# Order of the three partial products in a split-precision block, of a pass's first tile, and of four transposes at the start

## The chip, the cores and the metric

The kernel runs on one core of a Trainium2 chip. The metric is device time in microseconds (us) of one execution. The engines are named as the profile names them: PE is TensorE's matmul, PEld its weight load, DVE is VectorE, ACT is ScalarE, POOL is GpSimd, SP is SyncE. Here SP and POOL mostly issue DMA.

## The reference

One encoder layer on a float32 input x of 1024 tokens by 1024 features, weights of float32:

```python
h = swiglu(rmsnorm(x, ffn1_pre_g), ffn1_w_gate, ffn1_w_up, ffn1_w_down)   # 1024 -> 2816 -> 1024
x = x + 0.5 * rmsnorm(h, ffn1_post_g)
qkv = rmsnorm(x, mix_pre_g) @ w_qkv                                       # 16 heads of 64
# 8 heads: 2-D neighbourhood attention; 8 heads: three dilated windows, merged
x = x + rmsnorm(concat([rmsnorm(o_na), rmsnorm(o_dil)]) @ w_out, mix_post_g)
h = swiglu(rmsnorm(x, ffn2_pre_g), ffn2_w_gate, ffn2_w_up, ffn2_w_down)
x = x + 0.5 * rmsnorm(h, ffn2_post_g)
```

`swiglu(x, g, u, d)` is `(silu(x @ g) * (x @ u)) @ d`.

## The kernel before, in words

**Split numbers.** A float32 operand is held as two tiles of TensorE's rounded format: `hi`, the rounded value (an ACT cast), and `lo`, what the rounding lost (a DVE subtraction that reads `hi`). A product is three matmuls: hi times hi, hi times lo, lo times hi. `mm3` (L352) issues them in that order, on lines L354, L355 and L356; each loads its own 128x128 weights. In this kernel the tokens stream as moving operand and the weight columns stand in the array, so L356 is the only one of the three that needs the `lo` part of a weight.

**Seven products.** The large products follow a seven-multiplication scheme of two-by-two blocks. `PairGemm` (L429) does those whose weights stand: the gate and up projections of both feed-forward parts (22 blocks of 128 output columns each) and the q and k projection (8 blocks). `PairGemm.mm` (L457) does one block against one of the seven operands: four k of 128 rows, three matmuls each, so twelve matmuls into one PSUM bank. After the second and the fourth k it calls `c.step()`, which takes one waiting piece of work from each of two lists and issues it there; transposes of the next token tiles get into PE's queue in this way. `PairGemm.ahead` (L489) does the first `early` blocks (11, or all 8 of q and k) against the first two operands before the others exist; in its first turn it uses three blocks that `begin` in `layer` started. `split_left` makes hi and lo of a later block's weights with lines L453 (ACT) and L454 (DVE), called `graw` before and `whi`, `wlo` after. `save` copies a finished block out (L472) and stores it to DRAM (L529, tile `s1d`); the sink adds the second product into the same SBUF tile (DVE, L657), which must wait until that store has read it, and applies Silu (ACT, L659).

**Passes.** `Passes` (L707) does the products whose two sides both stream from DRAM: seven passes over chunks of 128 rows, in groups of up to four chunks (the last may have three or seven). In a group, for each of four token tiles t, it runs over the group's chunks with `mm3` and steps after every second chunk. The chunks' hi and lo (`pw`) are made in pairs on L737 (ACT) and L738 (DVE).

**Operands.** `Operand` (L186) normalises token tiles and transposes them; `one(t)` does half a tile: four PE transposes (L174), an ACT cast to hi, a DVE subtraction to lo, for some tiles a copy that is kept (L261) and stored.

**Order.** PE's instructions stand in the order in which the program issues them. On DVE and ACT a scheduler orders them from the program and its own estimate of when an input is ready; only in the opening (`begin`) are these two also kept in program order. So a new order on PE can move rows on ACT and DVE.

**The opening.** Tiles 0 to 3 are normalised and transposed first. Blocks 0 and 1 start with tiles 0 and 1 alone (256 columns), then take tiles 2 and 3, then block 2 takes all 512 columns. Meanwhile the right halves of the four tiles (operand A12) are transposed: two of them through the step list within block 1, one between blocks 1 and 2, one within block 2. Then `ahead` goes on with A12 for blocks 0 and 1, and with block 3, whose weights are the first that `split_left` makes.

Of the kernel before, what the change touches and what calls it, by code (L numbers as in the profile page):

```python
# [19 lines left out]
P, T = 128, 512  # L20
# [331 lines left out]
def mm3(c, out, ahi, alo, bhi, blo, start, stop, go_on=False):  # L352
    nc = c.nc
    nc.tensor.matmul(out, ahi, bhi, start=start, stop=False, skip_group_check=go_on)  # L354
    nc.tensor.matmul(out, ahi, blo, start=False, stop=False, skip_group_check=go_on)  # L355
    nc.tensor.matmul(out, alo, bhi, start=False, stop=stop, skip_group_check=go_on)  # L356
# [9 lines left out]
def nat_bank(c):  # L366
    return c.psm.tile([P, T], F32, tag="mm", name="accp")
# [61 lines left out]
class PairGemm:  # L429
# [27 lines left out]
    def mm(self, ps, w, i, a, go_on=False, cols=slice(0, T), ks=range(4)):  # L457
        hi, lo = w
        xhi, xlo = self.op.x[a]
        for k in ks:  # L460
            sl = slice(k * P, (k + 1) * P)
            mm3(self.c, ps[:, cols], hi[:, i, sl], lo[:, i, sl], xhi[:, k, cols], xlo[:, k, cols],
                not go_on and k == 0, k == 3, go_on)
            if k % 2:
                self.c.step()

    def bank(self):
        return self.c.psm.tile([P, T], F32, tag="mm", name="mmp")
# [238 lines left out]
class Passes:  # L707
# [35 lines left out]
    def run(self, *which, upto=6):  # L743

        c = self.c
        for p in which:
            chained = PASSES[p][0] in CHAINED
            if not chained:
                self.acc = [None] * 4
            acc, groups = self.acc, self.groups[p]  # L750
            for gi, g in enumerate(groups):
                while self.todo and self.todo[0][0] <= upto and len(self.ready) < len(g) + 3:
                    self.fetch()
                ops = [self.ready.popleft() for _ in g]
                end = gi == len(groups) - 1
                for t in range(4):
                    if acc[t] is None:
                        acc[t] = c.psm.tile([P, T], F32, tag="mm", name="accp")
                    sl = slice(t * P, (t + 1) * P)
                    for j, ((ahi, alo), (bhi, blo)) in enumerate(ops):  # L760
                        mm3(c, acc[t], ahi[:, sl], alo[:, sl], bhi, blo, not chained and gi == 0 and j == 0,
                            end and j == len(ops) - 1, chained)
                        if j % 2:
                            c.step()
                    if end:
                        self.take(p, t, acc[t])
                    c.tick()
# [574 lines left out]
def layer(tc, a, out):  # L1342
    nc = tc.nc
    c = Ctx(tc)
    with ExitStack() as ctx:
# [3 lines left out]
        def sub():  # L1349
            return ctx.enter_context(ExitStack())  # L1350
# [76 lines left out]
        def ffn(which, op, prep, pg, get, turns, sums, more, post, pre, src, dst, begin=None, tables=()):  # L1427
# [131 lines left out]
        with ExitStack() as order:  # L1559
# [16 lines left out]
            op0 = Operand(c, None, 0)  # L1576
# [8 lines left out]
            def begin(pg):  # L1585
# [63 lines left out]
                keeps = []  # L1649
# [13 lines left out]
                acc, s1 = [pg.bank() for _ in range(3)], []  # L1663
# [170 lines left out]
        with ordered():  # L1834
            ops = sub()
# [44 lines left out]
        with ordered():  # L1880
# [113 lines left out]
```

## Time and profile before

| what | us |
|---|---|
| time, median of 3 runs (1842.95 to 1844.0) | 1843.02 |
| the profiled execution: its time | 1842.29 |
| the profiled execution: its span in the trace | 1840.3 |
| PE busy, share of the span | 99% |
| DVE, ACT, POOL busy, share of the span | 72%, 45%, 18% |
| mean granted clock of PE over the span | 0.998 |

The span runs from the first to the last instruction of the program; the execution's time has 2.0 us beside it. A timeline row gives start, length, engine, line, operation, output tile and inputs, and in square brackets how long the engine sat idle before it and what it waited for. A row of waits gives total, number of times and the longest. Matmuls are pipelined, so a row's length is latency; the pace is the distance of starts.

### The profile page before, as it was taken

The numbers are of one execution on the slowest core, as the hardware profiler recorded it, in microseconds if no ns is written. First come the engines' busy times: TensorE is split into PE (matmuls) and PEld (weight loads), VectorE is DVE, ScalarE is ACT, GpSimd is POOL, SyncE is SP. The second block draws the span as 40 slices with busy tenths as digits, with TensorE's granted clock in tenths as the row PEclk, the third lists the DMA queues.
The fourth block names the chain that finished last, engine by engine and source line by source line (L and its number), as shares of the span: only waits on it lengthen the run. The fifth ranks groups of instructions, "written<-read, shape, count | busy, mean of one in ns | idle before, by whom it ended". The sixth has DMA issues, their size and how long they took to land.

```text
span 1840.3 us, 25143 instructions
## 1 busy us (share of the span) xinstructions
PE 1817.0 (99%) x8904; PEld 1527.5 (83%) x8904; DVE 1329.6 (72%) x2243; ACT 829.9 (45%) x1479; POOL 322.4 (18%) x508
## 2 busy tenths in 40 slices
PE   7999999999999999999999999999999999999998
PEld 6887888888888888888899998878888888888886
DVE  5878877776566877477777866778888777754557
ACT  6622233334443657133688765564222333354433
POOL 2223211111121122132333100121111111110000
PEclk9999999999999999999999999999999999999999
DMA  7756565657888857869686532595556566596564
GB/s 274 240 176 226 170 227 208 222 184 252 315 295 314 285 198 260 275 209 305 201 276 217 183 125 94 184 311 183 178 169 212 191 218 233 183 343 204 186 226 150
DMA packets 172991, 409.66 MB, mean 223 GB/s; under 512 B 20081, under 2 KB 42513, under 8 KB 170818
## 3 DMA queue, kind: packets, MB, share of 16 engines
q1 hardware_dynamic: 124706, 246.33, 40.6%
q0 software_dynamic: 47152, 159.64, 23.7%
q10 hardware_dynamic: 1008, 2.10, 0.3%
q8 instruction: 70, 1.15, 0.3%
q14 instruction: 55, 0.45, 0.1%
HBM read 280.49 MB, written 132.56 MB: 224 GB/s over the span
## 4 chain that ended last, share of the span: by engine, by line
PE 89%; DVE 4%; ACT 2%; issue 2%; DMA 2%; POOL 0%; SPq 0%; DVEq 0%; POOLq 0%; ACTq 0%
PE mmp L356 17%; PE mmp L354 17%; PE mmp L355 17%; PE accp L354 10%; PE accp L356 10%; PE accp L355 10%; PE po L1161 2%; PE po L1274 2%; PE ptp L1057 2%; PE trp L174 1%; PE sp L1258 1%; PE sp L1140 1%; DVE pw L738 1%; ACT pb L1049 1%; DMA s1d<-s 0%
## 5 line engine op out<-in xcount | busy, mean ns | idle before, releaser
L354 PE MATMUL mmp<-x,whi 128*128 128x512 f32 (+1 forms) x1464 | 572.7, 391 | 1.7 <-ACT whi L453 1.1
L356 PE MATMUL mmp<-x,wlo 128*128 128x512 f32 (+1 forms) x1464 | 570.2, 389 | 3.8 <-DVE wlo L454 3.8
L355 PE MATMUL mmp<-x,whi 128*128 128x512 f32 (+1 forms) x1464 | 570.1, 389 | 0.5 <-DVE x L182 0.3
L356 PEld LDWEIGHTS mmp<-x,wlo 128*128 128x128 f32 x1464 | 276.2, 189 | 62.2 <-DVE wlo L454 5.5
L354 PEld LDWEIGHTS mmp<-x,whi 128*128 128x128 f32 x1464 | 276.1, 189 | 59.9 <-issue 1.7
L355 PEld LDWEIGHTS mmp<-x,whi 128*128 128x128 f32 x1464 | 276.2, 189 | 56.9 <-DVE x L182 1.2
L738 DVE TENSOR_TENSOR pw<-praw,pw 128x1024 fp32r<-128x1024 f32 (+1 forms) x181 | 200.4, 1151 | 122.4 <-ACT pw L737 121.9
L737 ACT CAST pw<-praw 128x1024 fp32r<-128x1024 f32 (+1 forms) x181 | 168.4, 981 | 204.7 <-PE accp L356 167.7
L354 PE MATMUL accp<-pw 128*128 128x512 f32 x600 | 234.4, 391 | 0.0
L356 PE MATMUL accp<-pw 128*128 128x512 f32 x600 | 233.6, 389 | 0.0
L355 PE MATMUL accp<-pw 128*128 128x512 f32 x600 | 233.5, 389 | 0.0
L453 ACT CAST whi<-wraw 128x1024 fp32r<-128x1024 f32 x126 | 132.4, 1053 | 221.3 <-PE mmp L355 182.9
L454 DVE TENSOR_TENSOR wlo<-wraw,whi 128x1024 fp32r<-128x1024 f32 x126 | 154.6, 1229 | 20.5 <-ACT whi L453 19.2
L356 PEld LDWEIGHTS accp<-pw 128*128 128x128 f32 x600 | 112.6, 188 | 23.5
L355 PEld LDWEIGHTS accp<-pw 128*128 128x128 f32 x600 | 112.7, 188 | 23.2
L354 PEld LDWEIGHTS accp<-pw 128*128 128x128 f32 x600 | 112.7, 188 | 23.2 <-ACT hb L781 0.2
L453 ACT CAST whi<-traw 128x512 fp32r<-128x512 f32 x52 | 32.3, 622 | 157.6 <-DVE traw L545 104.4
L680 POOL DMA_DIRECT2D g<-sg x44 | 23.9, 543 | 428.6 <-DVE sg L673 239.9
L632 DVE TENSOR_TENSOR c<-mmp,u 128x512 f32<-128x512 f32 x52 | 35.9, 691 | 72.8 <-PE mmp L356 72.7
L472 ACT COPY s<-mmp 128x512 f32<-128x512 f32 x52 | 30.6, 588 | 121.3 <-PE mmp L356 113.9
L544 DVE TENSOR_TENSOR wraw<-wraw 128x1024 f32<-128x1024 f32 x52 | 63.6, 1223 | 13.1 <-DMA wraw<-in_wu_dram 12.2
L619 DVE TENSOR_TENSOR c<-mmp,v 128x512 f32<-128x512 f32 x52 | 35.7, 686 | 32.5 <-PE mmp L356 32.5
(286 smaller groups left out, 2775.4 us busy)
## 6 DMA issues: line engine op xcount, KB each, us to landing
praw<-g SPq DMA_DIRECT2D x70, 512.0 KB, 5.7
wraw<-in_wg_dram SPq DMA_DIRECT2D x44, 512.0 KB, 4.2
wraw<-in_wu_dram SPq DMA_DIRECT2D x44, 512.0 KB, 6.8
tr<-in_wd_dram SPq DMA_DIRECT2D x44, 512.0 KB, 6.6
g<-sg POOLq DMA_DIRECT2D x88, 256.0 KB, 5.0
ts<-tr POOLq DMA_DIRECT2D x22, 1024.0 KB, 4.7
praw<-ts SPq DMA_DIRECT2D x88, 256.0 KB, 3.8
praw<-in_wd_dram SPq DMA_DIRECT2D x66, 256.0 KB, 5.6
```

Source lines behind the costliest of these rows:

```text
L354: nc.tensor.matmul(out, ahi, bhi, start=start, stop=False, skip_group_check=go_on)
L355: nc.tensor.matmul(out, ahi, blo, start=False, stop=False, skip_group_check=go_on)
L356: nc.tensor.matmul(out, alo, bhi, start=False, stop=stop, skip_group_check=go_on)
L453: nc.scalar.copy(hi, raw)
L454: nc.vector.tensor_sub(lo, raw, hi.bitcast(F32))
L544: nc.vector.tensor_sub(r[:, 0:2], r[:, 1:3], r[:, 0:2])
L632: c.behind(lambda: nc.vector.tensor_add(c21, d, u2), *((DVE,) if self.sink.soon and b == self.n - 1 else ()))
L737: nc.scalar.copy(hi, raw[:, :m])
L738: nc.vector.tensor_sub(lo, raw[:, :m], hi.bitcast(F32))
L1057: nc.tensor.transpose(ps[:, j, :], src[:, j * P:(j + 1) * P], c.ident)
L1161: nc.tensor.matmul(po[:, un * 2 + j], pt[:, 2 * j + t, :], rhs, start=t == 0, stop=t == 1)
L1274: nc.tensor.matmul(po[0][:, u], pt[0][:, j, :], vs[:, k0 + j, :], start=j == 0, stop=j == n - 1)
```

## The change

It has three parts. In `PairGemm.mm` the twelve matmuls of a block are issued as eight with the `hi` weight (for each k: times x hi, times x lo) and then four with the `lo` weight. The first step comes after k = 1 of the `hi` ones, so after four matmuls in place of six; the second after all twelve, as before. In `Passes.run` the first token tile (t = 0) of a group takes its chunks two at a time: both chunks' hi times hi, both hi times lo, both lo times hi, with a step after each two and one more after an odd last chunk; the other three tiles are as before. In the opening, `one(2)` and `one(3)` of the right halves go into the step list of block 2 together, where `one(2)` was issued ahead of block 2.

```diff
     def mm(self, ps, w, i, a, go_on=False, cols=slice(0, T), ks=range(4)):
...
         for k in ks:
             sl = slice(k * P, (k + 1) * P)
-            mm3(self.c, ps[:, cols], hi[:, i, sl], lo[:, i, sl], xhi[:, k, cols], xlo[:, k, cols],
-                not go_on and k == 0, k == 3, go_on)
-            if k % 2:
+            mm(out, hi[:, i, sl], xhi[:, k, cols], start=not go_on and k == 0, stop=False, skip_group_check=go_on)
+            mm(out, hi[:, i, sl], xlo[:, k, cols], start=False, stop=False, skip_group_check=go_on)
+            if k == 1:
                 self.c.step()
+        for k in ks:
+            sl = slice(k * P, (k + 1) * P)
+            mm(out, lo[:, i, sl], xhi[:, k, cols], start=False, stop=k == 3, skip_group_check=go_on)
+        if 3 in ks:
+            self.c.step()
...
-                    for j, ((ahi, alo), (bhi, blo)) in enumerate(ops):
-                        mm3(c, acc[t], ahi[:, sl], alo[:, sl], bhi, blo, not chained and gi == 0 and j == 0,
-                            end and j == len(ops) - 1, chained)
-                        if j % 2:
+                    n = 2 if t == 0 else 1
+                    for j in range(0, len(ops), n):
+                        two = [(a[:, sl], b) for i in (0, 1, 2) for (ahi, alo), (bhi, blo) in ops[j:j + n]
+                               for a, b in [((ahi, bhi), (ahi, blo), (alo, bhi))[i]]]
+                        for i, (a, b) in enumerate(two):
+                            c.nc.tensor.matmul(acc[t], a, b, start=not chained and gi == 0 and j == i == 0,
+                                               stop=end and j + n >= len(ops) and i == len(two) - 1,
+                                               skip_group_check=chained)
+                        if n == 2 or j % 2:
                             c.step()
...
                 for b in range(3):
-                    if b == 1:
-                        c.steps.extend(lambda t=t: op0.one(t) for t in range(2))
-                    elif b:
-                        op0.one(2, keeps)
-                        c.steps.append(lambda: op0.one(3, keeps))
+                    if b:
+                        c.steps.extend(lambda t=t: op0.one(t, *([keeps] if t > 1 else [])) for t in (2 * b - 2, 2 * b - 1))
                     pg.mm(acc[b], pg.w[b], 0, A11, cols=slice(256 if b < 2 else 0, 512))
```

In the changed kernel L463 and L464 are the matmuls with the `hi` weight (L354 and L355 before) and L469 those with the `lo` weight (L356). Outside the touched functions' lines, its line numbers are higher by 6, later by 11 or 8: L657 and L659 become L663 and L665.

**First place: PE in the opening, end of block 2** (`x_161`, `x_162` are hi and lo of operand A11; `x_163`, `x_164` those of A12; `trp` is a transpose's output). Before, from the transposes of tile 3:

```order
L174 MATMUL trp<-ident,x 128x128 x4
L354 MATMUL mmp<-x_161,whi 128x512
L355 MATMUL mmp<-x_162,whi 128x512
L356 MATMUL mmp<-x_161,wlo 128x512
L354 MATMUL mmp<-x_161,whi 128x512
L355 MATMUL mmp<-x_162,whi 128x512
L356 MATMUL mmp<-x_161,wlo 128x512
L354 MATMUL mmp<-x_163,whi 128x512
L355 MATMUL mmp<-x_164,whi 128x512
```

With the change, from the transposes of tile 2:

```order
L174 MATMUL trp<-ident,x 128x128 x4
L463 MATMUL mmp<-x_161,whi 128x512
L464 MATMUL mmp<-x_162,whi 128x512
L463 MATMUL mmp<-x_161,whi 128x512
L464 MATMUL mmp<-x_162,whi 128x512
L469 MATMUL mmp<-x_161,wlo 128x512 x4
L174 MATMUL trp<-ident,x 128x128 x4
L463 MATMUL mmp<-x_163,whi 128x512
L464 MATMUL mmp<-x_164,whi 128x512
```

Tile 3's transposes moved behind block 2's last matmul, straight ahead of the first matmul that reads all of A12; the six matmuls that stood between them now stand ahead.

**Second place: ACT, a few instructions later** (`s_362` and `s_399` are the saved blocks 0 and 1; the first `whi<-graw` is block 3, the second block 4; L166 takes the squares of token tiles 4 and 5, then 6). Before:

```order
L261 COPY raw<-trp 128x512 x2
L166 ACTIVATE xn,ss<-x 128x1024 x2
L659 ACT_TABLE_LOAD
L659 ACTIVATE s_362<-s_362 128x512
L453 CAST whi<-graw 128x1024
L659 ACTIVATE s_399<-s_399 128x512
L166 ACTIVATE xn,ss<-x 128x1024
L453 CAST whi<-graw 128x1024
```

With the change:

```order
L261 COPY raw<-trp 128x512 x2
L166 ACTIVATE xn,ss<-x 128x1024 x2
L453 CAST whi<-graw 128x1024
L665 ACT_TABLE_LOAD
L665 ACTIVATE s_362<-s_362 128x512
L453 CAST whi<-graw 128x1024
L665 ACTIVATE s_399<-s_399 128x512
L166 ACTIVATE xn,ss<-x 128x1024
```

Block 3's cast moved ahead of a table load and the first Silu, block 4's ahead of the second Silu and a square.

**Third place: DVE, the same stretch** (L157 to L159 are steps of the reciprocal root for tiles 4 and 5, L226 scales these tiles). Before:

```order
L158 TENSOR_TENSOR e<-e,y 128x2
L657 TENSOR_TENSOR s_399<-mmp,s_399 128x512
L159 SCALAR_TENSOR_TENSOR y<-e,y 128x2
L226 SCALAR_TENSOR_TENSOR xn<-x,y,gain 128x1024
L454 TENSOR_TENSOR wlo<-graw,whi 128x1024
L226 SCALAR_TENSOR_TENSOR xn<-x,y,gain 128x1024
L454 TENSOR_TENSOR wlo<-graw,whi 128x1024
```

With the change:

```order
L151 TENSOR_SCALAR y<-y 128x2
L454 TENSOR_TENSOR wlo<-graw,whi 128x1024
L157 TENSOR_TENSOR e<-y,v 128x2
L158 TENSOR_TENSOR e<-e,y 128x2
L159 SCALAR_TENSOR_TENSOR y<-e,y 128x2
L663 TENSOR_TENSOR s_399<-mmp,s_399 128x512
```

Block 3's subtraction moved from behind the addition into `s_399` and one scaling to a place ahead of the iteration and of that addition.

More of the change, by code (lines that the diff above doesn't have):

```diff
@@ L459, in mm @@
         xhi, xlo = self.op.x[a]
+        mm, out = self.c.nc.tensor.matmul, ps[:, cols]
         for k in ks:
             sl = slice(k * P, (k + 1) * P)
-            mm3(self.c, ps[:, cols], hi[:, i, sl], lo[:, i, sl], xhi[:, k, cols], xlo[:, k, cols],
-                not go_on and k == 0, k == 3, go_on)
-            if k % 2:
+            mm(out, hi[:, i, sl], xhi[:, k, cols], start=not go_on and k == 0, stop=False, skip_group_check=go_on)
+            mm(out, hi[:, i, sl], xlo[:, k, cols], start=False, stop=False, skip_group_check=go_on)
+            if k == 1:
                 self.c.step()
+        for k in ks:
[3 more added lines that the diff above has]
+            self.c.step()
     def bank(self):
```

## The prediction

> **What bounds the kernel now.** I read the page's first part, then PE's waits, then one steady stretch by windows.
>
> ```profile
> PE 1817.0 (99%) x8904; PEld 1527.5 (83%) x8904; DVE 1329.6 (72%) x2243; ACT 829.9 (45%) x1479; POOL 322.4 (18%) x508
> PE mmp L356 <- DVE wlo L454: 3.8, 4, 2.6
> PE mmp L354 <- ACT whi L453: 1.1, 1, 1.1
> PE trp L174 <- ACT raw L261: 0.5, 1, 0.5
> L354 PE MATMUL mmp<-x,whi 128*128 128x512 f32 x1448 | 567.0, 392 | 1.1 <-ACT whi L453 1.1
> 1400.00:1500.00 100.00, 100.00 (x443) 82.83 (x442) 74.91 (x93) 34.25 (x46) 15.15 (x26) 1.00 0.62 216
> ```
>
> PE is busy for 99% of the span. The rows of waits give total, times and longest; the two `mmp` rows are the largest that an engine causes, 3.8 and 1.1 us. The window shows the rest: 443 matmuls in 100 us, so 0.226 us from start to start, at a granted clock of 1.00 (the number after POOL's). The other engines have slack. So a change can save only where PE stands still or its pace changes, and PE's stops of this kind lie in few places. The largest is at the opening:
>
> ```profile
> 32.56 0.39 PE L356 MATMUL mmp<-x,wlo 128*128 128x512 f32 x1
> 32.94 1.03 ACT L453 CAST whi<-graw 128x1024 fp32r<-128x1024 f32 x1
> 34.02 0.50 PE L354 MATMUL mmp<-x,whi 128*128 128x512 f32 x1 [1.06 <-ACT whi L453]
> 34.04 0.69 DVE L657 TENSOR_TENSOR s<-mmp,s 128x512 f32<-128x512 f32 x1 [0.77 <-DMA s1d<-s]
> 34.35 0.40 PE L355 MATMUL mmp<-x,whi 128*128 128x512 f32 x1
> 34.83 1.28 DVE L226 SCALAR_TENSOR_TENSOR xn<-x,y,gain 128x1024 f32<-128x1024 f32 x1
> 36.03 1.22 DVE L454 TENSOR_TENSOR wlo<-graw,whi 128x1024 fp32r<-128x1024 f32 x1
> 37.31 0.50 PE L356 MATMUL mmp<-x,wlo 128*128 128x512 f32 x1 [2.56 <-DVE wlo L454]
> 37.64 0.39 PE L354 MATMUL mmp<-x,whi 128*128 128x512 f32 x1
> 41.98 0.40 PE L354 MATMUL mmp<-x,whi 128*128 128x512 f32 x1
> 44.94 0.39 PE L355 MATMUL mmp<-x,whi 128*128 128x512 f32 x1
> ```
>
> Starts 0.226 apart are the pace; what is over it is lost. From 32.56 to 34.02 PE loses 1.23 us: block 3's first matmul waits for its ACT cast, which began only at 32.94. The second matmul comes 0.33 later, so 0.10 is lost in restarting. Then the first `lo` matmul is due at 34.58 and starts at 37.31: 2.73 lost, and 0.10 again behind it. The brackets show less idle time (1.06, 2.56), because the last matmul's latency counts as busy; so a wait costs its bracket and about 0.27. Why `lo` is late stands in the DVE rows: an addition into `s` waited 0.77 us for the store that reads this tile, and the scaling at 34.83 and the subtraction at 36.03 are queued behind it. From 37.64 to 41.98 are twelve starts, 2.72 us at the pace, but 4.34 passed: 1.62 more. Windows of 3.4 us say why (columns: us, busy of PE, PEld, DVE, ACT, POOL, then clock):
>
> ```profile
> 30.70:34.10 3.40, 2.33 (x11) 1.60 (x10) 2.12 (x13) 3.24 (x5) 1.15 (x3) 1.00 1.03 421
> 34.10:37.50 3.40, 0.84 (x3) 0.41 (x4) 3.37 (x5) 2.61 (x4) 1.02 (x2) 1.00 1.02 369
> 37.50:40.90 3.40, 3.40 (x11) 2.66 (x11) 2.09 (x2) 0.10 (x1) 0.00 (x0) 0.63 1.03 411
> ```
>
> After a stretch with PE busy for only 0.84 of 3.40 us the granted clock fell to 0.63. The stop at 34.02 to 37.31 is paid twice. All this sums to 1.23 + 0.10 + 2.73 + 0.10 + 1.62 = 5.8 us.
>
> The Trainium skill ("TensorE: Matmul & The Clock Gate", Part 1) says that the clock halves after an idle window of about 3.4 us, free-running, and warns of gaps over about 3.4 us. The trace does not agree in the size: a gap of 2.56 us idle, with few matmuls around it, was enough here. By the rule alone the 1.62 us would not be there to win and the sum below would be 5.3 us in place of 6.9; the measurement decides.
>
> **The change, part by part: the opening.** The order rows put tile 3's transposes behind block 2. What that costs is worked out from these rows:
>
> ```profile
> 23.54 0.42 PEld L174 LDWEIGHTS trp<-ident,x 128*128 128x128 f32 x4 [0.26 <-ACT raw L261]
> 25.42 0.60 PE L174 MATMUL trp<-ident,x 128*128 128x128 f32 x4
> 25.77 0.48 PE L354 MATMUL mmp<-x,whi 128*128 128x512 f32 x1
> 26.05 0.59 ACT L181 CAST x<-trp 128x512 fp32r<-128x512 f32 x1 [0.44 <-PE trp L174]
> 25.88 1.49 DVE L182 TENSOR_TENSOR x<-trp,x 128x512 fp32r<-128x512 f32 x2
> 27.25 0.39 PE L354 MATMUL mmp<-x,whi 128*128 128x512 f32 x1
> 27.47 0.45 PE L355 MATMUL mmp<-x,whi 128*128 128x512 f32 x1
> ```
>
> Up to the first A12 matmul (27.25) PE does the same work in both kernels. Tile 2's transposes waited 0.26 us at 23.54 for their PSUM buffer's copy; they now come four matmuls later, so this goes. Tile 3's slot is 0.35 (25.42 to 25.77). So in the changed kernel tile 3's transposes start at 27.25 - 0.26 - 0.35 = 26.64. Their output was there 0.63 after the start (26.05 - 25.42), the cast takes 0.59, and a subtraction 0.69 (25.88 + 1.49 = 27.37 is the end of two), with 0.10 to the matmul that reads it (27.47). That gives 27.27, 27.90, and with 0.03 between cast and subtraction 28.62 for the second's end: the first A12 matmul starts near 27.9, the second near 28.7, against 27.47 before. **This part costs 1.2 us**: a wait for the cast and one for the subtraction, in place of a wait of 0.2. Behind PE nothing is lost that isn't counted; on ACT the next copies, squares and block 3's cast stand behind the cast:
>
> ```profile
> 27.93 1.08 ACT L261 COPY raw<-trp 128x512 f32<-128x512 f32 x2
> 28.88 1.09 ACT L166 ACTIVATE xn<-x 128x1024 f32<-128x1024 f32 x1
> 30.88 0.21 ACT L166 ACTIVATION_READ_ACCUMULATOR xn<-x 128x1 f32 x1
> 31.11 1.28 ACT L659 ACT_TABLE_LOAD   x1
> 32.40 0.63 ACT L659 ACTIVATE s<-s 128x512 f32<-128x512 f32 x1
> graw<-in_wg_dram SPq DMA_DIRECT2D x1, 512.0 KB, 8.0
> ```
>
> The copies (1.08) follow a save (0.59, like the cast) and then begin at 28.5, not 27.93; the squares end near 31.7, not 31.09. In the changed order block 3's cast comes next, ahead of table load (1.28) and Silu (0.63). Its data, issued at 23.50, landed 8.0 us later, at 31.5. So `hi` is ready at 31.7 + 1.03 = 32.7, and `lo` (1.22, no longer behind the addition) at 34.0. PE reaches block 3 after 24 matmuls of A12: 28.7 + 0.10 + 23 x 0.226 = 34.0, its first `lo` eight later, 35.8. Both are in time, by 1.3 and 1.8 us, and this holds down to the next ones: block 4's cast follows the Silu (32.7 + 1.28 + 0.63 + 1.03 = 35.7, needed at 39.4). With no stop near 34 I expect no fall of the clock. Counting block 3's first matmul as one, the row at 44.94 is the 29th (12 of block 3, 12 of block 2's A12, 5 of block 4). Without the transposes that now stand shortly ahead of it, it starts at 34.0 + 28 x 0.226 = 40.3. **The opening gains 4.6 us**, the 5.8 less 1.2.
>
> **Three waits for `lo` later.** Each stands at a block's third matmul:
>
> ```profile
> 690.24 0.50 PE L356 MATMUL mmp<-x,wlo 128*128 128x512 f32 x1 [0.15 <-DVE wlo L454]
> 1202.56 0.50 PE L356 MATMUL mmp<-x,wlo 128*128 128x512 f32 x1 [0.40 <-DVE wlo L454]
> 1231.72 0.50 PE L356 MATMUL mmp<-x,wlo 128*128 128x512 f32 x1 [0.70 <-DVE wlo L454]
> 1230.45 1.22 DVE L454 TENSOR_TENSOR wlo<-graw,whi 128x1024 fp32r<-128x1024 f32 x1
> ```
>
> `lo` is now read six matmuls later, 6 x 0.226 = 1.36 us. The losses are the brackets and 0.27 each: 0.42, 0.67 and 0.97. All are below 1.36, so all three go, **2.1 us**. The third is the closest: PE arrives there earlier by the 0.67 saved just before, while the `lo` at 1230.45 hangs on a chain that I can't shift for sure; but the changed DVE order also puts it ahead of one 128x512 subtraction (0.69 in the row at 34.04), which pays that back.
>
> **A pass's first tile.**
>
> ```profile
> 733.30 0.39 PE L356 MATMUL mmp<-x,wlo 128*128 128x512 f32 x1
> 733.53 0.39 PE L354 MATMUL accp<-pw,x 128*128 128x512 f32 x1
> 734.52 0.50 PE L355 MATMUL accp<-pw,x 128*128 128x512 f32 x1 [0.61 <-DVE pw L738]
> ```
>
> The second matmul waits for `pw`'s `lo`; due at 733.76, it lost 0.76. One `hi` matmul now stands between: **0.23 us** gained. The rows of waits name no other pass that waits for an operand, so the pairs give nothing elsewhere: their `lo` is made while the group before is multiplied.
>
> **Moved for nothing.** A put's first half comes two matmuls (0.45 us) earlier, one in the last group before q and k comes six earlier, and some neighbours on ACT, DVE, SP (two loads of `wu` ahead of `wd`) and POOL change places. I take 0. The nearest row is the 0.5 us that one transpose waited for an ACT copy, the only such wait of an operand's put behind the opening; that one stays, since neither its place nor its ACT neighbours change. The other puts' tiles were scaled in time, which is what hides the move. If that cover failed in all eleven first halves it would cost 11 x 0.45 = 5.0 us; a swap of neighbours gives or costs at most one 0.69 row where PE waits for it, and I know of no such place but the one above.
>
> **Sum.** 4.6 + 2.1 + 0.2 = 6.9 us off the profiled execution's own 1842.29 (1840.3 of span and 2.0 around it): 1835.4. The median of the runs shown is 0.7 above that execution, so I predict **1836.1**.
>
> **Rivals.**
> - *The clock falls anyway.* The new waits at 27.9 and 28.7 stop PE for some 1.2 us. Against it: the window 30.70 to 34.10 had PE busy for 2.33 of 3.40 and the next one still started at clock 1.00. For it: the window's phase isn't in my hands. Price 1.6: 1837.7.
> - *Block 3's `hi` takes the place of `lo`.* If copies and squares run later than I have them, PE waits for the cast; it is in front of table load and Silu for certain, so the loss is at most the 1.23 of before and some restart, perhaps again at block 4: 1.5 to 2.5 lost, 1837.6 to 1838.6.
> - *The gain is given back.* The opening runs ahead, but the puts that come earlier find their tiles not yet scaled, and pay the 5.0 above: 6.9 - 5.0 = 1.9 is left, 1841.1, no difference. For it: the tiles are scaled on DVE, the second busiest engine (72%). Against it: none but the one put waited.
> - *Slower: the pace.* The change touches 3 x 1448 matmuls of full width in blocks. If eight with `hi` and four with `lo` run at another distance than 0.226, the whole span moves: 1.6 ns more each eats the 6.9, and from 2.4 ns on the kernel is slower by over 0.2% (3.7 us); at 2.5 ns it costs 10.9: 1847.0. Against it: from 733.30 to 733.53, from a `lo` weight to a `hi` one of another product, it is 0.23 like the mean of the window, in which same and other weights follow each other; and there is one weight load for each matmul (8904 of both), so no load repeats more or less than before.
> - *It doesn't do what it says.* PE would have to wait at the first `hi` matmul for `lo` as well; the order of PE's rows names `lo` only in the last four. Chance 0.
>
> **How the numbers follow.** Forecast 0.68, clock 0.08, `hi` in place of `lo` 0.09, given back 0.12, pace 0.03. Faster by over 0.2%, which is about what a measurement here can tell from no change, covers the first three: 0.85; within it 0.12; slower 0.03. The range reaches from 1834.0 (the opening's wait half as long, a put's 0.5 gone, the run-to-run spread) up to 1839.8, which takes in the clock and the late `hi`, and leaves out most of the last two.
>
> **What would show it.** Right: no PE wait for `wlo` or `whi` at blocks; two new short ones near 28 us, for L181 and L182; clock 1.00 throughout 30 to 42 us; the 29th matmul above at about 40.8 with the transposes ahead of it, not 44.94; the pace still 442 or 443 matmuls in 100 us. Wrong: a clock below 1 in the opening, a wait for `whi` near 34, a new wait at puts, or 440 matmuls in 100 us.

## The result, and the profile after

The changed kernel took 1837.24 us (median of 8 runs, 1836.51 to 1840.07), the kernel before 1843.0 (8 runs, 1840.68 to 1844.82): a ratio of 0.9969, 95% interval 0.996 to 0.9978. It is faster by 5.8 us, where 6.9 were forecast; 1836.1 was forecast and 1834.0 to 1839.8 was the range. Two further comparisons of the same kernel gave 0.9963 (0.9951 to 0.9976) and 0.9971 (0.996 to 0.9981).

The first part of the page and PE's waits (total, times, longest) in the changed kernel:

```profile
PE 1814.7 (99%) x8904; PEld 1525.1 (83%) x8904; DVE 1323.8 (72%) x2243; ACT 834.5 (45%) x1479; POOL 323.5 (18%) x508
```
```profile
PE mmp L463 <- ACT x L181: 1.3, 2, 0.7
PE mmp L463 <- DVE v L606: 1.1, 1, 1.1
...
PE mmp L464 <- DVE x L182: 0.6, 2, 0.4
```

No wait for a block's `whi` or `wlo` is left. The rows with L181 and L182 count two waits each: one stood before the change too, between 11 and 20 us, and the other is the one that the forecast put near 28 us. The row with `v` (L606) was not forecast. The pace did not move; the same steady window as before:

```profile
1400.00:1500.00 100.00, 100.00 (x443) 82.80 (x442) 74.10 (x92) 35.11 (x46) 14.60 (x25) 1.00 0.62 221
```

The opening in the timeline, PE's rows and the ACT and DVE rows that make block 3's weight:

```profile
26.57 0.51 PE L463 MATMUL mmp<-x,whi 128*128 128x512 f32 x1 [0.67 <-ACT x L181]
27.29 0.50 PE L464 MATMUL mmp<-x,whi 128*128 128x512 f32 x1 [0.22 <-DVE x L182]
30.69 1.05 ACT L453 CAST whi<-graw 128x1024 fp32r<-128x1024 f32 x1 [0.63 <-DMA graw<-in_wg_dram]
31.76 1.28 ACT L665 ACT_TABLE_LOAD   x1
31.77 1.22 DVE L454 TENSOR_TENSOR wlo<-graw,whi 128x1024 fp32r<-128x1024 f32 x1 [0.48 <-ACT whi L453]
32.64 0.39 PE L463 MATMUL mmp<-x,whi 128*128 128x512 f32 x1
34.45 1.07 PE L469 MATMUL mmp<-x,wlo 128*128 128x512 f32 x4
41.98 0.50 PE L463 MATMUL mmp<-x,whi 128*128 128x512 f32 x1
```

The cast starts at 30.69, when its data is there, ahead of the table load at 31.76; `wlo` ends at 32.99. PE reaches block 3 at 32.64 and its first `wlo` matmul at 34.45, and waits for neither. The matmul at 41.98 comes about 0.35 late, behind a copy of a bank (L478) that itself waited for a store; this was not forecast (0.50 and 0.39 in the two repeats). The clock (the number after POOL's) stays at 1.00:

```profile
34.00:37.40 3.40, 3.40 (x17) 2.82 (x15) 3.23 (x10) 2.19 (x4) 1.59 (x3) 1.00 1.00 374
37.40:40.80 3.40, 3.40 (x18) 2.83 (x17) 1.87 (x3) 0.00 (x0) 0.00 (x0) 1.00 1.02 411
```

To see where the time came from, I count PE's matmuls and transposes in order and take the time from the start of one to the start of another, at places where all kernels have done the same work. Each column is one stretch (from the n-th to the m-th; the first is counted from the span's start, and the last column is the start of the last one); the names are explained with the experiments below. `before 2` is a second profile of the kernel before; `after`, `after 2` and `after 3` are three of the changed one.

```
us, from n       0     44   2000   3004   3048   6100   6228   6260   8700
      to m      44    200   2100   3048   3240   6148   6260   6444   8790   last start
before       18.91  36.95  22.75   9.53  42.69  11.82   7.26  40.08  20.40      1832.40
before 2     18.67  37.39  23.22   9.56  42.69  11.80   6.92  40.09  21.08      1833.42
after        17.59  32.68  23.42   9.12  42.48  11.08   6.27  41.88  21.32      1828.09
after 2      18.07  32.92  22.67   9.47  42.47  11.10   6.27  42.04  20.71      1827.06
after 3      17.67  32.68  22.81   9.12  42.48  11.11   6.27  42.27  21.17      1827.54
e1           17.73  34.80  23.61   9.12  42.51  11.09   6.27  42.34  20.94      1830.07
e2           18.75  32.29  23.03   9.57  42.69  11.80   7.32  40.09  21.14      1829.54
e4           17.94  35.20  22.91   9.55  42.70  11.80   7.05  40.09  21.10      1829.99
f4           18.80  32.58  22.99   9.11  42.49  11.09   6.27  42.48  21.14      1828.93
g2           18.83  32.28  23.38   9.11  42.48  11.09   7.52  40.81  21.18      1828.51
g3           18.19  32.79  23.23   9.43  42.47  11.09   8.09  40.32  21.24      1828.52
h1           18.22  32.81  24.37   9.11  42.48  11.09   6.27  40.84  20.40      1827.54
h2           17.75  32.27  23.44   9.43  42.47  11.11   6.27  41.40  21.17      1828.00
```

Means of the three profiles after less the two before: start -1.01, opening (44 to 200) -4.41, the wait at 690 -0.31, the pass's first tile -0.22, the waits at 1202 and 1231 -0.71 and -0.82, then **+1.98** in the stretch behind them (6260 to 6444, 1235 to 1275 us of before). All else, the long steady stretches included, is +0.15. The sum is -5.35, of the profiles; the runs' medians differ by 5.8, with an interval of 4.1 to 7.4.

The start's -1.01 does not come from the change. The trace records the granted clock only from where it first rises to 1.00, at 15.31 us in `after`; a window ahead of that reads 1.00 because nothing is recorded there. Up to that point PE runs at half pace (rows at the end of this document), and the start follows the time of the rise in all 13 profiles (us):

```
              after 3  after     h2     e1     e4  after 2     g3     h1  before 2  before     g2     e2     f4
clock rises     15.19  15.31  15.73  15.79  16.05    16.50  16.56  16.70     17.60   17.91  18.00  18.13  18.31
44th starts     17.67  17.59  17.75  17.73  17.94    18.07  18.19  18.22     18.67   18.91  18.83  18.75  18.80
```

Kernels with the old order of the products rise early (e4) and late (e2), and so do those with the new one. In g2, whose opening is the changed kernel's, and in e2, which has its puts, the clock rose as late as in the kernel before. Their start and opening together take 51.11 and 51.04, the kernel before 55.86 and 56.06: 4.9 less, where the means above give 5.4. By this estimate some 4.8 of the 5.35 are the change's.

### The profile page after: what moved, and what is told of

It reads as the page before. It is cut to its first block, busy times and chain, and to the rows that moved or that the text cites. A ratio compares the mean times of both kernels' runs of the same rounds, so it can differ in the third digit from the quotient of the medians.

```text
span 1836.0 us, 25149 instructions
## 1 busy us (share of the span) xinstructions
PE 1814.7 (99%) x8904; PEld 1525.1 (83%) x8904; DVE 1323.8 (72%) x2243; ACT 834.5 (45%) x1479; POOL 323.5 (18%) x508
## 3 DMA queue, kind: packets, MB, share of 16 engines
q8 instruction: 70, 1.15, 0.2%
## 4 chain that ended last, share of the span: by engine, by line
PE 57%; issue 29%; DVE 4%; POOL 3%; DMA 3%; ACT 2%; POOLq 0%; SPq 0%; DVEq 0%; ACTq 0%
PE accp L771 13%; PE mmp L463 10%; PE mmp L464 10%; PE mmp L469 10%; PE po L1172 2%; PE po L1285 2%; PE ptp L1068 2%; PE accp L354 1%; PE accp L356 1%; PE accp L355 1%; POOL g L710 1%; PE sp L1269 1%; DVE pw L744 1%; PE sp L1151 1%; PE trp L174 1%
## 5 line engine op out<-in xcount | busy, mean ns | idle before, releaser
L463 PE MATMUL mmp<-x,whi 128*128 128x512 f32 (+1 forms) x1464 | 571.8, 391 | 2.6 <-ACT x L181 1.3
L464 PE MATMUL mmp<-x,whi 128*128 128x512 f32 (+1 forms) x1464 | 569.0, 389 | 0.7 <-DVE x L182 0.6
L771 PE MATMUL accp<-pw 128*128 128x512 f32 x1800 | 411.6, 390 | 1.1 <-DVE hb L805 0.6
L469 PE MATMUL mmp<-x,wlo 128*128 128x512 f32 (+1 forms) x1464 | 390.3, 388 | 0.0
L463 PEld LDWEIGHTS mmp<-x,whi 128*128 128x128 f32 x1464 | 275.6, 188 | 61.7 <-ACT x L181 2.2
L464 PEld LDWEIGHTS mmp<-x,whi 128*128 128x128 f32 x1464 | 275.7, 188 | 57.2 <-DVE x L182 1.6
L469 PEld LDWEIGHTS mmp<-x,wlo 128*128 128x128 f32 x1464 | 274.5, 188 | 56.7
L453 ACT CAST whi<-wraw 128x1024 fp32r<-128x1024 f32 x126 | 132.5, 1052 | 180.2 <-PE mmp L464 166.2
L453 ACT CAST whi<-traw 128x512 fp32r<-128x512 f32 x52 | 32.3, 621 | 135.2 <-DVE traw L551 91.5
L478 ACT COPY s<-mmp 128x512 f32<-128x512 f32 x52 | 30.6, 589 | 133.0 <-PE mmp L469 121.3
L771 PE MATMUL accp<-pw,x 128*128 128x512 f32 x312 | 71.9, 390 | 0.4 <-DVE pw L744 0.4
L771 PEld LDWEIGHTS accp<-pw,x 128*128 128x128 f32 x312 | 58.3, 188 | 12.8 <-DVE pw L744 0.8
L625 DVE TENSOR_TENSOR c<-mmp,v 128x512 f32<-128x512 f32 x52 | 35.8, 689 | 36.9 <-PE mmp L469 36.9
L1285 PE MATMUL po<-vs,pt 128*128 128x128 f32 x352 | 49.9, 276 | 0.0
L1068 PE MATMUL ptp<-ident,pb 128*128 128x128 f32 x304 | 48.9, 272 | 0.0
```

The lines of the kernel that those rows point to most:

```text
L453: nc.scalar.copy(hi, raw)
L463: mm(out, hi[:, i, sl], xhi[:, k, cols], start=not go_on and k == 0, stop=False, skip_group_check=go_on)
L464: mm(out, hi[:, i, sl], xlo[:, k, cols], start=False, stop=False, skip_group_check=go_on)
L469: mm(out, lo[:, i, sl], xhi[:, k, cols], start=False, stop=k == 3, skip_group_check=go_on)
L771: c.nc.tensor.matmul(acc[t], a, b, start=not chained and gi == 0 and j == i == 0, stop=end and j + n >= len(ops) and i == len(two) - 1, sk ...
L1068: nc.tensor.transpose(ps[:, j, :], src[:, j * P:(j + 1) * P], c.ident)
```

## The experiments

**e1 and e2: the change in two halves.** A put is the transposes of one token tile with what ACT and DVE make of their output; head's puts are those of the right halves in the opening. e1 is the changed kernel with head's puts as before; e2 is the kernel before with head's puts as changed, that is, the same edit the other way round:

```diff
-                    if b:
-                        c.steps.extend(lambda t=t: op0.one(t, *([keeps] if t > 1 else [])) for t in (2 * b - 2, 2 * b - 1))
+                    if b == 1:
+                        c.steps.extend(lambda t=t: op0.one(t) for t in range(2))
+                    elif b:
+                        op0.one(2, keeps)
+                        c.steps.append(lambda: op0.one(3, keeps))
```

> The changed kernel with head's puts as before (tile 2 ahead of block 2's first product, tile 3 at its first step); the new order of the products and of a pass's first tile stays. ACT and DVE then have the order of the kernel before around block 3. Theory A (the puts' place, through the order on ACT and DVE, is what saves the opening): PE still waits about 1.2 us for block 3's whi near 34 us, and for wlo about 1.35 in place of 2.73, since lo is read six matmuls later; with the 2.1 of the three later waits and 0.2 of a pass's first tile that is 3.7 us below the kernel before if the clock falls again, 5.3 if it doesn't (ratio 0.998 or 0.997). Theory B (the later reading of lo saves the opening by itself): no wait near 34, 8.1 us below (ratio 0.9956).

> The kernel before with head's puts in the new place alone; products and passes in the old order. ACT and DVE have the changed kernel's order around block 3. Theory A: no wait for whi near 34, the clock stays at 1.00, tile 3's new waits near 28 us cost 1.2; the opening gains about 4.3, less up to 0.5 where lo is read six matmuls earlier; the three later waits for wlo (0.42, 0.67, 0.97 lost) stay: 3.8 to 4.3 us below the kernel before, ratio 0.9978. Theory B: the stop near 34 to 37 stays, and tile 3's 1.2 comes on top: 1.2 us slower, ratio 1.0007.

e1 took 0.9978 (0.9969 to 0.9986) of the kernel before, 3.7 us less; e2 0.9977 (0.9966 to 0.9987), 4.1 less. PE's rows in e1's opening with a wait, and the windows around the second:

```profile
32.74 0.50 PE L463 MATMUL mmp<-x,whi 128*128 128x512 f32 x1 [1.09 <-ACT whi L453]
36.92 1.20 PE L469 MATMUL mmp<-x,wlo 128*128 128x512 f32 x4 [2.07 <-DVE wlo L454]
```
```profile
34.00:37.40 3.40, 1.33 (x6) 0.82 (x5) 3.36 (x5) 2.60 (x4) 0.72 (x2) 1.00 1.03 383
37.40:40.80 3.40, 3.40 (x17) 2.79 (x16) 1.79 (x2) 0.58 (x1) 0.34 (x1) 1.00 1.03 402
```

And in e2's:

```profile
27.70 0.50 PE L354 MATMUL mmp<-x,whi 128*128 128x512 f32 x1 [0.67 <-ACT x L181]
28.42 0.50 PE L355 MATMUL mmp<-x,whi 128*128 128x512 f32 x1 [0.22 <-DVE x L182]
```

In e1 the waits for `whi` and `wlo` are both there, though `wlo` is read six matmuls later; in e2 neither is, though it is read as early as before. So the stop at block 3 goes by the puts' place, through the order that it gives ACT and DVE. Theory B falls. Two details of e1 were not as expected: `wlo` was late by 2.07 and not 1.35, since PE came to block 3 at 32.74 in place of 34.02 while `wlo` came only 0.4 earlier (36.9 for 37.3); and the clock stayed at 1.00. That e1 saved the 3.7 of theory A is partly luck: this figure was for a clock that falls (5.3 if it doesn't), and it had no term for the stretch from 6260, which is 2.3 longer here. In the table the opening is 2.4 shorter in e1, 4.9 in e2 and 4.4 in the whole change. The +1.98 stands in e1 (42.34) and not in e2 (40.09): it belongs to the new order of the products or of the passes, not to the puts.

**e4: the kernel before, with only the order on ACT and DVE changed** at block 3 (no matmul moves; `own` holds the last ACT and DVE instruction behind the split):

```diff
-                self.sink.first(b, a, True, s1, tie)
+                with ExitStack() as st:
+                    for i in own if b < len(begun) - 1 else ():
+                        st.enter_context(c.tc.issue_after(i))
+                    self.sink.first(b, a, True, s1, tie)
             c.tick()
+            if begun and b == 0:
+                c.behind(lambda: self.split_left(len(begun)), ACT)
+                own = [next(i for i in reversed(nc.cur_bb.bb.instructions) if i.engine == e) for e in (ACT, DVE)]
```

> The kernel before, with only block 3's cast and subtraction ordered ahead of the first Silus on ACT and of the first additions into s on DVE; no matmul moves. Theory A: whi is there at about 32.7, wlo at about 34.0; PE loses about 0.7 at the third matmul of block 3 and some restart in place of 4.2, the clock stays at 1.00: 4.9 us below the kernel before, ratio 0.9973. Theory B (the order on ACT and DVE matters little, the products' order does): no difference, ratio 1.000.

It took 0.9986 (0.9977 to 0.9995), 2.7 us less: half of it. PE's waits, and the ACT rows behind the second:

```profile
33.40 0.50 PE L356 MATMUL mmp<-x,wlo 128*128 128x512 f32 x1 [0.53 <-DVE wlo L454]
...
44.84 0.50 PE L354 MATMUL mmp<-x,whi 128*128 128x512 f32 x1 [2.52 <-ACT s L472]
```
```profile
33.52 1.06 ACT L453 CAST whi<-graw 128x1024 fp32r<-128x1024 f32 x1 [1.43 <-DMA graw<-in_wg_dram]
34.59 1.28 ACT L666 ACT_TABLE_LOAD   x1
...
44.20 0.59 ACT L472 COPY s<-mmp 128x512 f32<-128x512 f32 x1 [1.83 <-DMA sgd<-s]
```

The first half is as expected: the `whi` wait is gone, the `wlo` wait is 0.53, the clock stayed at 1.00. But the tie was too strong: block 4's cast went ahead of the table load too, and the first Silu came at 35.89 in place of 32.40. Its store left later, and a copy into the same tile (44.20) waited for it; PE lost 2.77 there. With no matmul moved, the order on ACT and DVE took away one stop of this size and made another.

**Repeats: e3 and i1, the changed kernel again; g4, the kernel before again.**

> The changed kernel as it is, for a second profile. Theory A: the opening repeats (no wait near 34, clock 1.00 from 30 to 42); the new waits of the first profile at 474.98 (0.46 idle), 1266.89 (1.15) and 1798.22 (0.64) hang on when transfers land; those that hang on the program's order repeat within 0.1, those that hang on how transfers meet come and go. Theory C (all of them belong to the change): all three repeat, and the time stays 4.3 us below the profiled execution of the kernel before.

> The changed kernel as it is, beside the other two on one chip, and for a third profile. The waits for L181 and L182 near 27, near 42 (0.3 to 0.5) and for v near 1266 (1.1 to 1.2 idle) repeat; those for hb near 475 and 1798 may be there or not (both kernels have shown them and not shown them).

> The kernel before as it is, for a second profile. Theory A: the waits at 34.02 (whi), 37.31 (wlo), 690.24, 1202.56 and 1231.72 repeat within 0.2, since they follow from the order on the engines; the clock falls again behind the stop near 37, as it did in the first profile (1.6 us). Theory H (the fall hangs on the phase of the clock's own windows, not on the stop alone): the stop is there and the clock stays at 1.00, with twelve starts behind it in 2.7 us in place of 4.3. The wait for the hb copy near 475 to 480 and near 1800 is absent, since PE comes there later.

(g4 took 0.9999 of the kernel before, 0.9989 to 1.0009.) In before, all five waits repeat, two of them not within the 0.2 that I gave (2.98 in place of 2.56 near 37, 0.37 in place of 0.70 near 1232), and the clock falls again. These two windows are the clock's own: in the trace's records it rises at 17.60 us, falls at 38.08 and rises at 41.49, that is, 6 and 7 times 3.413 us behind the first rise.

```profile
34.67:38.07 3.40, 0.57 (x3) 0.48 (x3) 3.36 (x5) 2.67 (x4) 0.63 (x2) 1.00 1.04 386
38.08:41.49 3.41, 3.41 (x10) 2.63 (x9) 1.70 (x2) 0.00 (x0) 0.00 (x0) 0.50 1.02 412
```

Theory H stays open: the first rise was at 17.91 and 17.60 in the two profiles, so the clock's windows lay nearly alike, and no profile shows this stop with another phase.

In the changed kernel the waits near 27 and 1266 repeat (for `v`: 1.15, 1.15 and 0.82 idle), and so does the small one near 42 (idle for 0.25 in the second profile, too short to be listed in the other two). The waits for `hb`, the tile that takes a pass's finished banks, near 475 and 1798 come and go; the kernel before has them in its second profile too (480.52, idle for 0.26), where I had expected none. They do not belong to the change, and theory C falls for them.

**g2 and h1: where the 1.98 comes from.** In this stretch the last early blocks of the second feed-forward part run, with the last put (token tile 7) among them. L310 is a subtraction of that put, for operand S3; L295 casts an operand's hi, L296 subtracts for its lo. `sg` is a block's Silu, `sgd` its copy in DRAM, `tr<-in_wd_dram` a load of `wd`, and `v` an SBUF tile to which DVE adds a finished bank. Rows of the changed kernel:

```profile
1250.45 1.28 DVE L296 TENSOR_TENSOR x<-s,x 128x512 fp32r<-128x512 f32 x2
1251.66 0.68 DVE L310 TENSOR_TENSOR s<-x,s 128x512 f32<-128x512 f32 x1
1252.37 0.63 ACT L295 CAST x<-s 128x512 fp32r<-128x512 f32 x1 [1.04 <-DVE s L310]
1252.91 0.58 ACT L665 ACTIVATE sg<-mmp 128x512 f32<-128x512 f32 x1
1253.02 0.55 SPq L413 DMA_DIRECT2D tr<-in_wd_dram  x1
1253.79 0.54 POOL L669 DMA_DIRECT2D sgd<-sg  x1 [1.61 <-ACT sg L665]
1260.17 0.60 ACT L665 ACTIVATE sg<-mmp 128x512 f32<-128x512 f32 x1 [1.98 <-DMA sgd<-sg]
1261.73 1.23 DVE L454 TENSOR_TENSOR wlo<-wraw,whi 128x1024 fp32r<-128x1024 f32 x1 [2.29 <-ACT whi L453]
1266.06 0.68 DVE L606 TENSOR_TENSOR v<-mmp,u 128x512 f32<-128x512 f32 x1
1266.89 0.47 PE L463 MATMUL mmp<-x,whi 128*128 128x512 f32 x1 [1.15 <-DVE v L606]
```

and of the kernel before, for the same work:

```profile
1255.73 0.68 DVE L310 TENSOR_TENSOR s<-x,s 128x512 f32<-128x512 f32 x1
1256.93 1.89 DVE L296 TENSOR_TENSOR x<-s,x 128x512 fp32r<-128x512 f32 x3
1258.30 0.54 POOL L663 DMA_DIRECT2D sgd<-sg  x1 [2.72 <-ACT sg L659]
1259.49 0.55 SPq L413 DMA_DIRECT2D tr<-in_wd_dram  x1
```

Before, the put's subtraction L310 stands ahead of the L296 subtractions. In the changed kernel it stands behind three of them; its ACT cast, which is ahead of the Silu, waits 1.04 for it, so the Silu's store is issued behind the two loads of `wd` and not ahead of them. It lands after 6.3 us (the changed kernel, first line) in place of 2.3 (before):

```profile
DMA to landing us min/median/max: 6.3/6.3/6.3
```
```profile
DMA to landing us min/median/max: 2.3/2.3/2.3
```

The later Silu at 1260.17 waits 1.98 for that tile, the cast and the `wlo` behind it are late, `v` is added late on DVE, and PE waits 1.15 for `v`'s bank. All 13 profiles agree: in the five with the store behind the loads it lands after 6.0 to 6.4 us, in the eight with the store ahead after 2.3. g2 issues that subtraction early in every put; h1 does the same under `if t == 7`, for the last tile alone:

```diff
-        c.sums.extend([lambda: (sub(s2, s1, a11), split(S2, s2)), lambda: split(S1, s1),
-                       lambda: (sub(a21, a11, a21), split(S3, a21)), end])
+        c.sums.extend([lambda: (sub(s2, s1, a11), sub(a21, a11, a21), split(S2, s2)), lambda: split(S1, s1),
+                       lambda: split(S3, a21), end])
```

> The changed kernel; in the second half of a put of tiles 4 to 7 the subtraction for S3 (L310) is issued right behind the one for S2 (L309), so that on DVE it comes ahead of two of the three L296 subtractions that stood before it. Theory D (the wait of 1.3 us at 1266 comes from this place: L310 late on DVE, its cast late on ACT, the Silu behind the cast late, so its store leaves behind the two loads of wd and lands 6.3 us later in place of 2.3, and the next Silu but one waits for the tile): the Silu at 1252.91 comes about 1.0 earlier, the store leaves ahead of the loads and lands after some 2.3 to 4 us, PE's wait for v falls from 1.15 to 0 to 0.3; 1.0 to 1.3 us below the changed kernel. Theory E (the wait comes from the new order of the products by itself, S4 reaching its bank before v is added): the wait stays at 1.1 to 1.3, no difference.

> The changed kernel; the early subtraction for S3 only in the put of tile 7, the last one, so that at tile 4's put DVE keeps the changed kernel's order (block's wlo ahead of three subtractions). Theory D (the two waits have separate places on DVE: at tile 4's put the subtraction ahead of wlo costs 1.0 near 1228, at tile 7's put the late one costs 1.3 near 1266): neither wait for wlo near 1228 nor for v near 1266; a loss of up to 0.5 near 1256 may come, as in the kernel with all four; about 1 us below the changed kernel. Theory I (PE catches up with DVE in this stretch, whatever the order, and what one place saves another takes): a wait of 0.7 to 1.3 elsewhere between 1220 and 1275; no difference.

g2 took 0.9978 (0.9969 to 0.9987). Its rows:

```profile
1226.79 1.22 DVE L454 TENSOR_TENSOR wlo<-graw,whi 128x1024 fp32r<-128x1024 f32 x1
1228.06 1.20 PE L469 MATMUL mmp<-x,wlo 128*128 128x512 f32 x4 [0.98 <-DVE wlo L454]
1254.38 0.54 POOL L669 DMA_DIRECT2D sgd<-sg  x1 [0.48 <-ACT sg L665]
1255.34 0.55 SPq L413 DMA_DIRECT2D tr<-in_wd_dram  x1
1260.02 0.59 ACT L665 ACTIVATE sg<-mmp 128x512 f32<-128x512 f32 x1
```

The store now leaves ahead of the loads, the later Silu waits for nothing, and the wait for `v` is gone: theory D holds, E falls. But at tile 4's put the early subtraction and the L296 rows went ahead of a block's `wlo` (1226.79; 1224.17 in the changed kernel), and PE waited 0.98 for it. h1 has neither wait, and the two stretches are 6.27 and 40.84, 1.2 us less than the changed kernel's mean. So 1.2 of the 1.98 comes from this place; 0.75 stays, 0.48 of it ahead of one matmul, where the changed kernel loses 0.18 to 0.28:

```profile
1256.39 0.50 PE L467 MATMUL mmp<-x,whi 128*128 128x512 f32 x1 [0.32 <-ACT s L482]
```

(In h1 and h2 these line numbers are higher by 4: L467 is L463, L482 is L478, L457 is L453.) The copy L482 stands on ACT behind a cast (L295) that waited 1.22 for another subtraction of the put (L299). Whether that order can be mended was not tried. h1's time was 0.9971 (0.9961 to 0.9981), equal to the changed kernel's on the same chip: 1.2 us is 0.07%, less than these runs can tell, and the profiled execution had 1.39 of wait for `hb` near 476, one of those that come and go.

**f4 and h2: is the new place of tile 3 needed?** f4 is e1 with the order on ACT and DVE tied as the changed kernel has it: only the first Silu behind block 3's cast, only the second addition into `s` behind its subtraction, so that block 4's cast stays behind the Silu. In `GatePairs.first`, with `own` from `ahead` as in e4 (ACT's instruction for b = 0, DVE's for b = 1):

```diff
+            if own is not None and b == 1:
+                add.enter_context(c.tc.issue_after(own))
             nc.vector.tensor_add(sg, ps, s1)
+            add.close()
             ps = sg
+        if own is not None and b == 0:
+            act.enter_context(c.tc.issue_after(own))
         c.behind(lambda: nc.scalar.activation(sg, ps, AF.Silu), *tie)
+        act.close()
```

g3 is f4 with g2's edit. h2 is f4 with h1's edit and with block 5's cast behind the copy of block 3:

```diff
-                self.c.behind(lambda: self.split_left(b + 1), *(self.sink.late if b else ()))
+                self.c.behind(lambda: self.split_left(b + 1), *((ACT,) if begun and b == len(begun) + 1 else self.sink.late if b else ()))
```

> The changed kernel with head's puts as before, but block 3's cast and subtraction ordered ahead of the first Silu on ACT and of the second addition into s on DVE, as the changed kernel has them. Theory F (the new place of tile 3 costs 1.4 us for nothing; the order on ACT and DVE is all that is needed): no waits for L181 and L182 near 27, block 3's whi late by at most 0.5; 0.9 us or more below the changed kernel. Theory G (the opening is bound by landings: the weight at 30.6 and the store of the first Silu at about 41.2, which a copy into the same tile waits for): the 1.4 come back as 0.5 at block 3 and as 0.8 to 1.0 more at the wait near 42; no difference to the changed kernel, ratio 0.9965 to the kernel before.

> The kernel with the early subtraction for tile 7 and, in the opening, head's puts as before with block 3's weight ordered ahead, and block 5's cast ordered behind the copy that PE waits for near 42. The store of the first Silu lands near 41.7, the copy takes 0.59: PE's wait near 42 falls from the 1.35 lost with the order of the other kernel to 0.5 to 0.8. Theory G (the opening is bound by landings): at most 0.5 us below the kernel with tile 7's edit alone. Theory F (the order was the fault): 0.9 or more below it.

> The two edits of the other kernels of this call together (the early subtraction for S3; head's puts as before with block 3's weight ordered ahead). If theories D and F hold: about 2.2 us below the changed kernel, 8.1 below the kernel before (ratio 0.9956). If D and G: 1.0 to 1.3 below the changed kernel. If E and G: no difference to the changed kernel.

f4 took 0.9966 (0.9954 to 0.9979), h2 0.9962 (0.995 to 0.9975), g3 0.9978 (0.9969 to 0.9988; it has g2's wait near 1228, 8.09 in the table, which none of its forecasts had). The opening's late wait in f4 with the ACT row ahead of it, then h2's waits and the ACT row of its block 3:

```profile
43.08 0.50 PE L463 MATMUL mmp<-x,whi 128*128 128x512 f32 x1 [1.10 <-ACT s L478]
...
41.49 1.05 ACT L453 CAST whi<-graw 128x1024 fp32r<-128x1024 f32 x1 [4.49 <-DMA graw<-in_wg_dram]
```
```profile
32.08 0.50 PE L467 MATMUL mmp<-x,whi 128*128 128x512 f32 x1 [0.41 <-ACT whi L457]
41.68 0.50 PE L467 MATMUL mmp<-x,whi 128*128 128x512 f32 x1 [0.23 <-ACT s L482]
...
30.98 1.05 ACT L457 CAST whi<-graw 128x1024 fp32r<-128x1024 f32 x1 [1.16 <-DMA graw<-in_wg_dram]
```

The waits for tile 3 near 27 are gone in both. f4 pays them back near 42, but not for the reason that theory G gave: the copy (L478) stood behind block 5's cast, which waited 4.49 for its data, and not for the Silu's store. With that order mended, h2 loses 0.23 there and 0.41 at block 3, whose cast waited for its data to land (30.98). So the cause that theory G names at block 3 holds. h2's opening is 32.27, 0.5 less than the changed kernel's mean of 32.76, as G allows; but g2, whose opening is the changed kernel's, has 32.28, so one profile of h2 does not show that the 0.5 is the order's. h2's median, 1836.57, is the lowest here; on its chip h1 took 1837.29 and the changed kernel 1837.51, and the intervals overlap. Between F and G the times do not decide. No version is shown to beat the changed kernel.

## Why the prediction was right, and where not

- **The opening: right.** 4.6 forecast, 4.4 measured; together with the start, at an equal rise of the clock, 4.9. The mechanism was the one named: block 3's cast and subtraction ahead on ACT and DVE. e2 shows that this comes from the puts' place alone, e1 that reading `wlo` later does not do it. Tile 3's cost was forecast at 1.2, after what the old place lost, and was 1.2: from the 44th of PE's instructions to the third matmul that reads A12 it is 10.0 to 10.1 us in the three profiles of the changed kernel and 8.85 in both of the kernel before. The new stops alone are 1.5: the transposes were issued by 25.65 and the first matmul came at 26.57 (0.92), the second 0.72 later in place of 0.226 (0.50), the third 0.34 later (0.11). Block 3 came at 32.64, not 34.0, since this profile's start was 1.3 shorter; the 29th matmul from there came 6.71 later (at 39.35), where 6.8 were forecast. One step was off without harm: block 3's cast was reckoned to begin behind ACT's squares, 0.2 after its data had landed, and it waited 0.63 for its data. Not forecast was the small loss near 42.
- **The clock: right.** 1.00 throughout. The kernel before loses this part in both its profiles. The page "TensorE: Matmul & The Clock Gate" of the Trainium skill (Part 1) wants about 3.4 us without work for a fall. Here the longest gaps were 2.56 and 2.98 us, and the fall came in both; by the rule alone the opening would have gained 3.0 (4.6 less 1.6), and it gained 4.4.
- **The three later waits and a pass's first tile: right.** 2.1 and 0.23 forecast; 0.31, 0.71 and 0.82, and 0.22 measured. The table shows that they belong to the new order of the matmuls: e1, with the old puts, has these gains, and e2, with the new puts alone, has none of them.
- **"Moved for nothing", taken at 0: wrong.** The stretch behind the three waits came out 2.0 longer. The bound of 5.0 held it, but the mechanism was none that I named: no tile was scaled late and PE did not wait at a put. A neighbour on DVE changed places, and it moved a store behind two loads; that is shown for 1.2 of the 2.0 (h1). The rule that a swap of neighbours costs at most one row of 0.69 was wrong with it. "I know of no such place" was a search in PE's waits only; the place was on DVE, and it reached PE through ACT, a store and DVE again. Of the rival "the gain is given back" only two fifths of the price came, and not by its mechanism.
- **The start: luck.** It was not forecast, and it was 1.0 shorter in the three profiles than in the two, because the clock rose earlier in them. It flatters the sum of the profiles by some 0.5. The 4.8 that is left lies within the runs' interval of 4.1 to 7.4; why the runs' medians differ by more, 5.8, stays open.
- **The pace: right.** 443 matmuls in the window; the stretch from 200 to 2000 took 406.81 to 406.87 us in all five profiles of the two kernels.

## What to carry to other kernels

When a change moves work on one engine and a scheduler orders the others, compare the order of every engine, and price the moves by what they push behind a transfer, not by their own length. A wait removed in one place moves the next limit closer: here a part of the gain met a landing or a queue that had been hidden. What a small reorder is worth is shown by a version that makes only the reorder on the other engines. Before two profiles are compared stretch by stretch, compare when the clock rose in each: here that alone moved the start by up to 1.3 us.

## What the runs showed of the hardware

- In the 13 traces the granted clock is recorded as 1.00 or 0.50, and it changes at whole multiples of 3.413 us from its first rise. So the 0.63 in the prediction's window is a mean across two of the clock's own: the record is 0.50 from 38.39 to 41.80 us. In these windows of its own the clock fell behind one in which PE was busy for 1.08 us (the kernel before) and one with 0.57 (its second profile). It did not fall behind windows with 1.99 (e1, waits of 1.09 and 2.07) and 1.92 (e4, one wait of 2.52). Where between 1.08 and 1.92 the limit lies was not tried. The rise asked for more: at the start it came behind windows with PE busy for 3.25 us or more, and not behind one with 3.09 (f4).
- A 256 KB store that was issued 1.0 to 1.2 us ahead of two loads of 512 KB landed in 2.3 us (eight profiles); the same store issued 0.8 us behind the first of them took 6.0 to 6.4 us (five).
- In the first 15 us of the changed kernel's first profile the 256-column matmuls start 0.213 us apart and later 0.119. The change comes with the first record of the clock, at 15.31; there is none before it:

```profile
14.82 0.41 PE L463 MATMUL mmp<-x,whi 128*128 128x256 f32 x1
15.03 0.41 PE L464 MATMUL mmp<-x,whi 128*128 128x256 f32 x1
...
18.70 0.28 PE L464 MATMUL mmp<-x,whi 128*128 128x256 f32 x1
18.82 0.28 PE L463 MATMUL mmp<-x,whi 128*128 128x256 f32 x1
```
